# Decoder layer, attention: the mean of squares between the next tile's transposes and its product with v, the normalised output in a tile of its own

## The chip, the cores and the metric

The kernel runs on one core of one Trainium2 chip. The metric is the device time of one execution in microseconds; before the change it is 1115.36 us, the median of three runs.

## The reference, cut to what matters

The kernel computes one decoder layer on 1024 tokens of width 1024, all in float32. A combined projection feeds two mixers, a differential attention group with 4 heads and a short gated convolution; their outputs are concatenated and projected, a layer norm follows, then a gated feed-forward block with a convolution and a second layer norm. The change touches the end of the attention alone:

```python
p = jax.nn.softmax(sc, axis=-1)
a = p[:, :, 0] - lam * p[:, :, 1]
o = einsum('bhqk,bhkd->bhqd', a, v)
...
o = o * lax.rsqrt(jnp.mean(jnp.square(o), axis=-1, keepdims=True) + RMS_EPS)
o = o * attn_norm_g * (1.0 - lam_init)
```

The mean is over the 128 columns of one head, for each query.

## The kernel before

**Tiling.** The four heads follow one another (`attention(h)`, line 380). A head first gets its q and k from a projection (`project`, `pair`, lines 339 and 99). Then the queries go in four tiles of 256, `c` = 0 to 3, each of two halves of 128, `qi` = 0 and 1. A half makes both score maps (lines 448 to 450, with the causal mask added by a matmul), takes the negated row maximum on VectorE (451), the exponential on ScalarE (455), the reciprocal of the sums (460) and the difference of the two softmaxes (463 on ScalarE, 464 on VectorE). Work grows with the causal length: from 128 to 1024 keys.

**Precision.** Float32 operands are split into a rounded high part (ScalarE, line 65) and a rest (VectorE, line 66), and a product is three matmuls (74, 75, 76). A tile named with h or l at its end is such a part.

**Spread and product with v.** `spread` (409) is deferred by one half through the list `post`: it transposes the softmax difference in groups of four blocks into the one PSUM bank `tp` (415), splits each group into `pa`, and at `qi` = 1 multiplies `pa` with v into `o`, a PSUM tile of tag `pv`, which has one buffer (420 to 424). `o` is transposed output: 128 head columns by 256 queries. It is copied to `osb` (426, one buffer), and the normalisation is put on the list `rms`.

**Normalisation.** `normalise` (357) is taken from `rms` at `qi` = 1 of the next tile (`RMS_AT`, line 457); the last tile of a head waits for tile 0 of the next head, and the very last comes after everything (519). It squares `osb` on VectorE (359), splits the square into `sqh` and `sql` (65, 66), and sums over the partitions with two matmuls by a matrix of 1/128 into `mq` (364, 365), which has the same single `pv` buffer as `o`. ScalarE reads `mq` (368) and takes the inverse root by a logarithm and an exponential (370, 371). GpSimd refines it with one Newton step, multiplies it with the norm's weights and with `osb` in place (373 to 377); for the very last tile VectorE does this. SyncE's queue then writes `osb` to `cat_d` in device memory (378), from where the output projection reads it back later (597). The tiles `me` and `y` use the buffers of `sq` and `sql`; each of these tags has one buffer.

**What sets the order.** Each engine works through its own list of instructions in order. The lists are made when the program is built: a scheduler walks the program with its own idea of durations, so the order on an engine is not the order of the source. Matmuls of convolution projections (`CONV`, line 511; they are the X and Z products) stand between those of the attention. A tile is allocated anew only when its buffer's last reader is through. `after(late, early)` (line 49) adds an order between two instructions without a wait on the chip.

Of the kernel before, what the change touches and what calls it, by code (L numbers as in the profile page):

```python
# [8 lines left out]
F32 = mybir.dt.float32  # L9
# [3 lines left out]
ALU = mybir.AluOpType  # L13
# [3 lines left out]
P = 128  # L17
# [11 lines left out]
QC = 256  # L29
# [14 lines left out]
def layer_kernel(ctx: ExitStack, tc: tile.TileContext, x, xt, w_in, w_v, lam, vecs, w_out, ln, w_up, w_down, out):  # L44
    nc = tc.nc
    V, A, T, G = nc.vector, nc.scalar, nc.tensor, nc.gpsimd
    SQ = nc.sync

    def after(late, early):

        tc.add_manual_dep(late.ins, early.ins.name, mybir.DependencyInfo(
            mybir.DependencyClass.NoSync, mybir.DependencyReason.DATA), reason="order")
# [9 lines left out]
    def split(hi, lo, src, scale=None, eng=None):  # L62

        if scale is None:
            A.copy(hi, src)  # L65
            (eng or V).tensor_tensor(lo, src, hi.bitcast(F32), op=ALU.subtract)  # L66
        else:
            A.mul(hi, src, scale)
            V.scalar_tensor_tensor(lo, src, scale, hi.bitcast(F32), op0=ALU.mult, op1=ALU.subtract)
# [79 lines left out]
    cat_d = [[dram.tile([P, 512], F32, name=f"cat_d{k}_{c}") for c in range(2)] for k in range(8)]  # L149

    ident = const.tile([P, P], F32, name="ident")
# [7 lines left out]
    ones = const.tile([P, P], F32R, name="ones")  # L159
# [165 lines left out]
    at = pool("at", ab, side="right")  # L325
# [26 lines left out]
        G.memset(kl[(1 - m) * DH:(2 - m) * DH].bitcast(F32), 0.0)  # L352
        klo.append(kl)

    rms, post = [], []

    def normalise(h, c, osb):
        sq = at.tile([P, QC], F32, name="sq", tag="sq")
        V.tensor_tensor(sq, osb, osb, op=ALU.mult)
        sqh = at.tile([P, QC], F32R, name="sqh", tag="sqh")  # L360
        sql = at.tile([P, QC], F32R, name="sql", tag="sql")
        split(sqh, sql, sq)
        mq = p_pv.tile([P, 512], F32, name="mq", tag="pv", bufs=1)
        T.matmul(mq[:, :QC], ones, sqh, start=True, stop=False)
        T.matmul(mq[:, :QC], ones, sql, start=False, stop=True)

        me = at.tile([P, QC], F32, name="me", tag="sq")
        A.activation(me, mq[:, :QC], AF.Identity, bias=epsc)
        y = at.tile([P, QC], F32, name="y", tag="sql")
        A.activation(y, me, AF.Ln)  # L370
        A.activation(y, y, AF.Exp, scale=-0.5)
        E = V if (h, c) == (H - 1, S // QC - 1) else G
        E.tensor_tensor(me, me, y, op=ALU.mult)
        E.tensor_tensor(me, me, y, op=ALU.mult)
        E.tensor_scalar(me, me, gm, gp, op0=ALU.mult, op1=ALU.add)
        E.tensor_tensor(y, y, me, op=ALU.mult)
        E.tensor_tensor(osb, y, osb, op=ALU.mult)
        SQ.dma_start(cat_d[h][c // 2][:, c % 2 * QC:(c % 2 + 1) * QC], osb)

    def attention(h):  # L380

        q2 = [qk.tile([P, S], F32R, name=f"q{m}_{h}", tag=f"q{m}") for m in range(2)]
        k2 = [qk.tile([P, S], F32R, name=f"k{m}_{h}", tag=f"k{m}") for m in range(2)]

        def put_q(cs, v):
            for m in range(2):
                a_, b_ = slice(m * DH, (m + 1) * DH), slice((1 - m) * DH, (2 - m) * DH)
                A.mul(q2[m][a_, cs], v[a_], DH ** -0.5)
                V.scalar_tensor_tensor(q2[m][b_, cs], v[a_], DH ** -0.5, q2[m][a_, cs].bitcast(F32),
                                       op0=ALU.mult, op1=ALU.subtract)  # L390

        def put_k(cs, v):
            for m in range(2):
                a_, b_ = slice(m * DH, (m + 1) * DH), slice((1 - m) * DH, (2 - m) * DH)
                A.copy(k2[m][a_, cs], v[a_])
                A.copy(k2[m][b_, cs], v[a_])
                V.tensor_tensor(klo[m][a_, cs], v[a_], k2[m][a_, cs].bitcast(F32), op=ALU.subtract)

        qa, qb, ka, kb = project(h, H + h)
        put_k(c1, kb)  # L400
        put_q(c1, qb)
        put_q(c0, qa)
        put_k(c0, ka)
        vhl = at.tile([P, 2, NT, P], F32R, name=f"vhl{h}", tag="vhl")
        for c in range(2):
            SQ.dma_start(vhl[:, c].bitcast(F32), v_d[c][:, h])
        vh, vl = vhl[:, 0], vhl[:, 1]

        def spread(c, qi, pm, pa):
            i, nkb = 2 * c + qi, 2 * c + 2  # L410
            for j0 in range(0, i + 1, 4):
                nj = min(4, i + 1 - j0)
                tp = p_tr.tile([P, 4, P], F32, name="tp", tag="tr", bufs=1)
                for j in range(nj):
                    T.transpose(tp[:, j, :], pm[0][:, (j0 + j) * P:(j0 + j + 1) * P], ident)
                g = pa[j0 // 4]
                split(g[:, 0, 0:nj, qi * P:(qi + 1) * P], g[:, 1, 0:nj, qi * P:(qi + 1) * P], tp[:, :nj, :])
            if qi == 0:
                return
            o = p_pv.tile([P, 512], F32, name="o", tag="pv", bufs=1)  # L420
            for j in range(nkb):
                qs = slice(P if j == nkb - 1 else 0, QC)
                mm3(o[:, qs], vh[:, j, :], vl[:, j, :], pa[j // 4][:, 0, j % 4, qs], pa[j // 4][:, 1, j % 4, qs],
                    j == 0, j == nkb - 1, skip_group_check=True)
            osb = at.tile([P, QC], F32, name="osb", tag="osb")
            A.copy(osb, o[:, :QC])
            rms.append(lambda: normalise(h, c, osb))

        for c in range(S // QC):
            nkb = 2 * c + 2  # L430
            pa = [at.tile([P, 2, 4, QC], F32R, name=f"pa{h}_{c}_{g}", tag="pa", bufs=2) for g in range((nkb + 3) // 4)]
            for qi in range(2):
                i = 2 * c + qi
                n = (i + 1) * P
                qs = slice(i * P, (i + 1) * P)
                if post:
                    post.pop(0)()
                nm = at.tile([P, 2], F32, name="nm", tag="nm", bufs=3)
                sm = at.tile([P, 2], F32, name="sm", tag="sm", bufs=3)
                pm = []  # L440
                for m in range(2):
                    if i >= 4 or m == 0:
                        sc_ = p_sc.tile([P, S], F32, name="sc", tag="sc", bufs=2)
                    sc = sc_[:, m * 512:] if i < 4 else sc_
                    for b0 in range(0, n, 512):
                        b1 = min(n, b0 + 512)
                        bs = slice(b0, max(b1, b0 + 256))
                        T.matmul(sc[:, bs], q2[m][:, qs], k2[m][:, bs], start=True, stop=False)  # L448
                        T.matmul(sc[:, bs], q2[m][:, qs], klo[m][:, bs], start=False, stop=b1 < n)
                    T.matmul(sc[:, qs], identb, maskb, start=False, stop=True)  # L450
                    V.tensor_reduce(nm[:, m:m + 1], sc[:, :n], axis=AX.X, op=ALU.max, negate=True)  # L451
                    if i >= 4 or m == 0:
                        pt_ = at.tile([P, S], F32, name=f"p{m}", tag="p", bufs=3)
                    pt = pt_[:, m * 512:] if i < 4 else pt_
                    A.activation(pt[:, :n], sc[:, :n], AF.Exp, bias=nm[:, m:m + 1], accum_out=sm[:, m:m + 1])  # L455
                    pm.append(pt)
                if rms and (c, qi) in RMS_AT:
                    rms.pop(0)()
                rc = at.tile([P, 2], F32, name="rc", tag="rc", bufs=3)
                V.reciprocal(rc, sm)  # L460
                cc = at.tile([P, 1], F32, name="cc", tag="cc", bufs=3)
                V.tensor_tensor(cc, rc[:, 1:2], nlam, op=ALU.mult)
                A.mul(pm[0][:, :n], pm[0][:, :n], rc[:, 0:1])
                V.scalar_tensor_tensor(pm[0][:, :n], pm[1][:, :n], cc, pm[0][:, :n],  # L464
                                       op0=ALU.mult, op1=ALU.add)
                post.append(lambda c=c, qi=qi, pm=pm, pa=pa: spread(c, qi, pm, pa))

    def convolve(j):
# [44 lines left out]
    for h in range(H):  # L513
# [3 lines left out]
        if post:  # L517
            post.pop(0)()
    rms.pop(0)()
    xop_st.close()  # L520


# [142 lines left out]
    early, gates = {}, {}  # L665
# [274 lines left out]
    for j in range(HK + 2):  # L940
        if j < HK:
            op = ready.pop(0) if ready else (operand(a11[j], "S", j), operand(b11[j], "T", j))
            for t in range(4):
                mm_row(X, op, t, j == 0, j == HK - 1)
        if j >= 2:
            i = j - 2
            op = (operand(add(a21[i], a22[i], ALU.add), "S", i),
                  operand(add(b12[i], b11[i], ALU.subtract), "T", i))
# [7 lines left out]
    for t in range(4):  # L956
# [5 lines left out]
            after={2 * i: (lambda i=i: thirds(NTHIRD + i)) for i in range(HK - NTHIRD)})  # L962
# [77 lines left out]
```

## Time and profile before

| what | value |
|---|---|
| median of 3 runs | 1115.36 us (1113.97 to 1116.62) |
| the profiled execution | 1116.29 us, its span 1114.5 us |
| TensorE busy | 1082.9 us, 97% of the span, 4988 matmuls |
| VectorE busy | 890.1 us, 80% |
| ScalarE busy | 504.7 us, 45% |
| GpSimd busy | 98.7 us, 9% |
| granted TensorE clock, mean | 0.996 |

The span runs from the first to the last instruction; 1.8 us of the execution lie outside it. Busy times of different engines overlap. A wait is put down to whatever came last by the profile. TensorE's matmuls are pipelined and their ends modelled, so what counts is the time between two starts and the idle time in front of one. PE stands for TensorE's matmuls, DVE for VectorE, ACT for ScalarE, POOL for GpSimd, SPq for SyncE's queue of transfers.

### The profile page before, as it was taken

Reading aid. Unit: us, or ns where it says so; the run is one execution under the profiler, and the core shown is the slowest. Engines: PE = TensorE matmul, PEld = TensorE weight load, DVE = VectorE, ACT = ScalarE, POOL = GpSimd, SP = SyncE. Lnnn points to the kernel's source line nnn. Section 1 sums busy time; section 2 is a strip of 40 time slices with the busy share of each in tenths; the row PEclk is TensorE's granted clock in tenths of the full one; section 3 lists DMA queues with packets and bytes.
Section 4 is the critical chain, followed back from the end, with each engine's and each line's share of the span. In section 5 each row is a group of like instructions: output and inputs, shape, how many; then the busy total and the mean of one; then the engine's idle time right before and its main releaser. Section 6 shows DMA issues by size and latency. Waiting matters only on the chain.

```text
span 1114.5 us, 13774 instructions
## 1 busy us (share of the span) xinstructions
PE 1082.9 (97%) x4988; PEld 877.4 (79%) x4988; DVE 890.1 (80%) x1380; ACT 504.7 (45%) x936; POOL 98.7 (9%) x147
## 2 busy tenths in 40 slices
PE   7998999999999999999999999999999999999997
PEld 5876777877767888888888888888888887788885
DVE  7777889779888777898777777777676599997797
ACT  6357577378577421254333333333333243444540
POOL 0002313112132021200000000000000000000102
PEclk9998999999999999999999999999999999999999
DMA  7531111221213675123212122222212294120112
GB/s 265 157 94 43 43 67 39 78 74 49 81 48 112 215 256 205 42 98 126 95 57 100 71 95 76 88 83 76 95 67 85 97 397 196 39 71 34 47 66 76
DMA packets 48692, 114.32 MB, mean 103 GB/s; under 512 B 4848, under 2 KB 15216, under 8 KB 48624
## 3 DMA queue, kind: packets, MB, share of 16 engines
q1 hardware_dynamic: 48624, 113.45, 28.5%
q8 instruction: 39, 0.64, 0.2%
q14 instruction: 29, 0.24, 0.1%
HBM read 86.69 MB, written 26.74 MB: 102 GB/s over the span
## 4 chain that ended last, share of the span: by engine, by line
PE 77%; DVE 11%; ACT 4%; DMA 3%; POOL 2%; issue 2%; SPq 0%; POOLq 0%; DVEq 0%; ACTq 0%
PE X L76 9%; PE X L74 9%; PE X L75 9%; PE Z L76 5%; PE Z L74 5%; PE Z L75 5%; PE op L75 3%; PE op L74 3%; PE op L76 3%; PE dx L75 3%; PE dx L76 2%; PE dx L74 2%; PE Y L74 2%; PE Y L76 2%; PE dz L74 2%; PE dz L76 2%
## 5 line engine op out<-in xcount | busy, mean ns | idle before, releaser
L66 DVE TENSOR_TENSOR a<-s,a 128x512 fp32r<-128x512 f32 x118 | 85.4, 725 | 50.1 <-ACT a L65 49.2
L65 ACT CAST a<-s 128x512 fp32r<-128x512 f32 x118 | 73.6, 624 | 100.8 <-PE X L76 48.4
L65 ACT CAST a<-w 128x512 fp32r<-128x512 f32 x106 | 65.9, 623 | 96.9 <-PE X L76 40.3
L66 DVE TENSOR_TENSOR a<-w,a 128x512 fp32r<-128x512 f32 x106 | 74.1, 701 | 16.2 <-ACT a L65 15.9
L65 ACT CAST T<-b 128x512 fp32r<-128x512 f32 x66 | 40.7, 622 | 68.4 <-PE dz L76 33.9
L75 PE MATMUL dx<-T,S 128*128 128x512 f32 x176 | 69.1, 393 | 1.2 <-DVE T L66 1.2
L76 PE MATMUL dx<-T,S 128*128 128x512 f32 x176 | 68.6, 390 | 0.0
L74 PE MATMUL dx<-T,S 128*128 128x512 f32 x176 | 66.0, 391 | 0.0
L66 DVE TENSOR_TENSOR T<-b,T 128x512 fp32r<-128x512 f32 x66 | 45.3, 689 | 16.6 <-ACT T L65 16.6
L451 DVE TENSOR_REDUCE nm<-sc 128x1 f32<-128x128 f32 (+5 forms) x64 | 47.5, 751 | 6.2 <-PE sc L450 5.7
L75 PE MATMUL dz<-T,S 128*128 128x512 f32 x132 | 51.8, 392 | 0.0
L76 PE MATMUL dz<-T,S 128*128 128x512 f32 x132 | 51.5, 390 | 0.0
L74 PE MATMUL op<-wo,c 128*128 128x512 f32 x128 | 50.6, 395 | 0.0
L455 ACT ACTIVATE p<-sc,nm 128x128 f32<-128x128 f32 (+5 forms) x64 | 47.5, 743 | 6.3 <-DVE p L464 3.8
L76 PE MATMUL op<-wo,c 128*128 128x512 f32 x128 | 50.0, 390 | 0.0
L75 PE MATMUL op<-wo,c 128*128 128x512 f32 x128 | 50.0, 390 | 0.0
L74 PE MATMUL dz<-T,S 128*128 128x512 f32 x132 | 48.4, 394 | 0.5 <-ACT T L65 0.4
L810 ACT ACTIVATE t<-t 128x1024 f32<-128x1024 f32 x22 | 23.4, 1062 | 50.7 <-DVE t L809 50.7
L448 PE MATMUL sc<-k,q 128*128 128x512 f32 (+2 forms) x96 | 37.1, 394 | 5.4 <-ACT p L455 4.6
L75 PEld LDWEIGHTS dx<-T,S 128*128 128x128 f32 x176 | 33.0, 188 | 9.7 <-DVE T L66 2.9
L74 PEld LDWEIGHTS dx<-T,S 128*128 128x128 f32 x176 | 33.0, 188 | 7.4 <-ACT T L65 0.6
L76 PEld LDWEIGHTS dx<-T,S 128*128 128x128 f32 x176 | 33.1, 188 | 6.7
(318 smaller groups left out, 3229.9 us busy)
## 6 DMA issues: line engine op xcount, KB each, us to landing
w<-in_w_up SPq DMA_DIRECT2D x44, 512.0 KB, 3.3
b<-in_w_down SPq DMA_DIRECT2D x44, 256.0 KB, 6.6
w<-in_w_in SPq DMA_DIRECT2D x20, 512.0 KB, 3.4
act_d<-act SPq DMA_DIRECT2D x19, 512.0 KB, 2.6
ra<-act_d SPq DMA_DIRECT2D x19, 512.0 KB, 7.1
v_d<-vs SPq DMA_DIRECT2D x16, 256.0 KB, 2.7
vhl<-v_d SPq DMA_DIRECT2D x8, 512.0 KB, 4.7
wo_r<-in_w_out SPq DMA_DIRECT2D x8, 512.0 KB, 3.9
```

Of the source, the lines that this page charges most:

```text
L65: A.copy(hi, src)
L66: (eng or V).tensor_tensor(lo, src, hi.bitcast(F32), op=ALU.subtract)
L74: T.matmul(ps, lh, rh, start=first, stop=False, **kw)
L75: T.matmul(ps, lh, rl, start=False, stop=False, **kw)
L76: T.matmul(ps, ll, rh, start=False, stop=last, **kw)
L448: T.matmul(sc[:, bs], q2[m][:, qs], k2[m][:, bs], start=True, stop=False)
L451: V.tensor_reduce(nm[:, m:m + 1], sc[:, :n], axis=AX.X, op=ALU.max, negate=True)
L455: A.activation(pt[:, :n], sc[:, :n], AF.Exp, bias=nm[:, m:m + 1], accum_out=sm[:, m:m + 1])
L810: A.activation(t_, t_, AF.Silu)
```

## The change

The normalisation is cut in two. `squares` makes `sq`, `sqh` and `sql` where `normalise` stood. The rest goes on a second list, `means`, and is taken from it inside the next `spread` with `qi` = 1, right after the first group of transposes, with an order that puts the first `mq` matmul behind the last of these transposes. In the source, its ScalarE and GpSimd work now comes ahead of the split of that group. The product with `osb` is now the first of the five GpSimd instructions and writes a new tile `on`, which has the one buffer of `sqh`; the last multiplies `on` by the refined factor, and the transfer reads `on`.

```diff
-    def normalise(h, c, osb):
+    def squares(h, c, osb):
         sq = at.tile([P, QC], F32, name="sq", tag="sq")
         V.tensor_tensor(sq, osb, osb, op=ALU.mult)
         sqh = at.tile([P, QC], F32R, name="sqh", tag="sqh")
         sql = at.tile([P, QC], F32R, name="sql", tag="sql")
         split(sqh, sql, sq)
+        means.append(lambda early=None: normalise(h, c, osb, sqh, sql, early))
+
+    def normalise(h, c, osb, sqh, sql, early):
         mq = p_pv.tile([P, 512], F32, name="mq", tag="pv", bufs=1)
-        T.matmul(mq[:, :QC], ones, sqh, start=True, stop=False)
+        first = T.matmul(mq[:, :QC], ones, sqh, start=True, stop=False)
+        if early is not None:
+            after(first, early)
...
         E = V if (h, c) == (H - 1, S // QC - 1) else G
+        on = at.tile([P, QC], F32, name="on", tag="sqh")
+        E.tensor_tensor(on, y, osb, op=ALU.mult)
         E.tensor_tensor(me, me, y, op=ALU.mult)
         E.tensor_tensor(me, me, y, op=ALU.mult)
         E.tensor_scalar(me, me, gm, gp, op0=ALU.mult, op1=ALU.add)
-        E.tensor_tensor(y, y, me, op=ALU.mult)
-        E.tensor_tensor(osb, y, osb, op=ALU.mult)
-        SQ.dma_start(cat_d[h][c // 2][:, c % 2 * QC:(c % 2 + 1) * QC], osb)
+        E.tensor_tensor(on, on, me, op=ALU.mult)
+        SQ.dma_start(cat_d[h][c // 2][:, c % 2 * QC:(c % 2 + 1) * QC], on)
...
                 for j in range(nj):
-                    T.transpose(tp[:, j, :], pm[0][:, (j0 + j) * P:(j0 + j + 1) * P], ident)
+                    last = T.transpose(tp[:, j, :], pm[0][:, (j0 + j) * P:(j0 + j + 1) * P], ident)
+                if qi == 1 and means:
+                    means.pop(0)(last)
...
-            rms.append(lambda: normalise(h, c, osb))
+            rms.append(lambda: squares(h, c, osb))
...
     rms.pop(0)()
+    means.pop(0)()
```

## Rows read from the trace of the kernel before

**Rows 1.** Page, part 1: busy time, share of the span, instructions.
```profile
PE   1082.9 (97%) x4988; PEld 877.4 (79%) x4988; DVE 890.1 (80%) x1380; ACT 504.7 (45%) x936; POOL 98.7 (9%) x147
```
**Rows 2.** Busy time by stretch: PE, PEld, DVE, ACT, POOL; clock; DMA share; GB/s.
```profile
85.00:385.00 300.00, 286.94 (x1452) 225.51 (x1451) 250.11 (x423) 198.39 (x416) 65.23 (x78) 0.99 0.21 73
102.20:105.69 3.49, 0.00 (x1) 0.00 (x0) 1.22 (x2) 1.99 (x4) 0.00 (x0) 0.86 0.54 188
105.69:111.60 5.91, 5.91 (x17) 4.64 (x18) 4.04 (x7) 2.55 (x6) 0.00 (x0) 0.50 0.00 0
197.00:213.00 16.00, 16.00 (x70) 12.89 (x69) 11.19 (x16) 5.51 (x10) 1.95 (x3) 1.00 0.22 74
370.00:400.00 30.00, 30.00 (x134) 24.74 (x133) 21.91 (x32) 5.07 (x8) 1.90 (x2) 1.00 0.57 215
```
**Rows 3.** Waits, 75 to 385 us: total us, times, longest us.
```profile
PE sc L448 <- ACT p L455: 4.6, 5, 1.5
PE mq L364 <- ACT sqh L65: 3.9, 2, 3.5
ACT osb L426 <- DMA cat_d<-osb: 11.3, 6, 3.4
DVE s L117 <- DMA w<-in_w_in: 1.0, 2, 0.5
```
**Rows 4.** Timeline, head 0, tiles 0 and 1: start us, duration us, engine.
```profile
92.44 0.28 PE L364 MATMUL mq<-sqh,ones 128*128 128x256 f32 x1
...
95.79 1.14 POOL L373 TENSOR_TENSOR me<-me,y 128x256 f32<-128x256 f32 x1 [51.53 <-DVE rc L460]
...
98.49 2.52 POOL L376 TENSOR_TENSOR y<-y,me 128x256 f32<-128x256 f32 x1
...
101.08 0.73 POOL L377 TENSOR_TENSOR osb<-y,osb 128x256 f32<-128x256 f32 x1
...
101.84 0.33 SPq L378 DMA_DIRECT2D cat_d<-osb  x1
...
103.66 0.37 ACT L426 COPY osb<-o 128x256 f32<-128x256 f32 x1 [3.37 <-DMA cat_d<-osb]
...
105.69 0.58 PE L364 MATMUL mq<-sqh,ones 128*128 128x256 f32 x1 [3.49 <-ACT sqh L65]
```
**Rows 5.** Timeline of PE: the other idle times behind a late osb.
```profile
121.30 0.55 PE L415 MATMUL tp<-ident,p 128*128 128x128 f32 x3 [0.65 <-DVE pa L66]
...
179.83 0.50 PE L448 MATMUL sc<-k,q 128*128 128x512 f32 x1 [1.43 <-ACT p L455]
...
263.26 0.39 PE L364 MATMUL mq<-sqh,ones 128*128 128x256 f32 x1 [0.46 <-ACT sqh L65]
...
334.71 0.50 PE L448 MATMUL sc<-k,q 128*128 128x512 f32 x1 [1.55 <-ACT p L455]
```
**Rows 6.** Groups of instructions, 85 to 385 us: busy us, mean ns; idle before.
```profile
L377 POOL TENSOR_TENSOR osb<-y,osb 128x256 f32<-128x256 f32 x15 | 14.6, 971 | 1.2
L368 ACT ACTIVATE me<-mq,epsc 128x256 f32<-128x256 f32 x16 | 7.6, 477 | 2.2 <-PE mq L365 2.1
L370 ACT ACTIVATE y<-me 128x256 f32<-128x256 f32 x16 | 6.7, 421 | 0.3
L377 DVE TENSOR_TENSOR osb<-y,osb 128x256 f32<-128x256 f32 x1 | 0.4, 419 | 0.0
```
**Rows 7.** Timeline, head 1: transposes of tiles 0, 1 and 2, and tile 1's loop.
```profile
161.53 0.38 PE L415 MATMUL tp<-ident,p 128*128 128x128 f32 x2
...
167.77 0.38 PE L415 MATMUL tp<-ident,p 128*128 128x128 f32 x2
...
180.39 0.28 PE L364 MATMUL mq<-sqh,ones 128*128 128x256 f32 x1
...
182.86 0.60 PE L415 MATMUL tp<-ident,p 128*128 128x128 f32 x4
...
188.97 0.36 ACT L426 COPY osb<-o 128x256 f32<-128x256 f32 x1
```

More of the change, by code (lines that the diff above doesn't have):

```diff
@@ L353, in layer_kernel @@
         klo.append(kl)
-    rms, post = [], []
-    def normalise(h, c, osb):
+    rms, means, post = [], [], []
+    def squares(h, c, osb):
         sq = at.tile([P, QC], F32, name="sq", tag="sq")
```

## The prediction

> **What bounds the kernel now.** I read the busy times first: TensorE is busy 97% of the span, the next engine 80% [rows 1]. So time is lost or won where TensorE stands still or runs slowly. The stretches come next: attention, from 85 to 385 us, leaves TensorE idle for 300 - 286.9 = 13.1 us [rows 2]. That, and what the clock loses, is all that a reordering inside attention can win.
>
> The waits say who ends this idle time: scores that wait for an exponential (4.6 us) and the mean's matmul that waits for `sqh` (3.9 us) [rows 3]. Behind both stands one wait on ScalarE: six copies of `o` to `osb` wait 11.3 us in all until the last tile's output has left the one `osb` buffer [rows 3]. ScalarE works in order, so exponentials and splits queue behind such a copy.
>
> The timeline shows it in full in head 0. The mean of tile 0 starts at 92.44, GpSimd starts at 95.79 and needs until 101.81, the write goes out at 101.84, and the copy of tile 1, which waited 3.37 us, runs at 103.66. TensorE has the mean's matmul next in its list and idles 3.49 us [rows 4]. Then the granted clock is 0.50 from 105.69 to 111.60, the lower of its two levels (1.2 of 2.4 GHz): 5.91 us of work that takes 2.95 us at the full clock [rows 2]. The other copies cost TensorE 0.65, 1.43, 0.46 and 1.55 us [rows 5]. The chain thus costs TensorE 3.49 + 4.09 = 7.58 us of idle time (0.67 us per us of ScalarE's wait) and 2.95 us of clock: **10.5 us** of the profiled 1116.29 us, which stands 0.9 us above the median of 1115.36.
>
> **What the change removes.** `osb` is now read for the last time by GpSimd's first instruction, not by the write behind the fifth. A mean of GpSimd's multiplication is 0.97 us [rows 6]; the buffer comes free some 6.0 - 1.1 + 1.8 = 6.7 us earlier after the root is there [rows 4]. Against that the mean starts later, behind the next tile's transposes. I take it that the wait for `osb` goes in all six places: -10.5 us, bounds -10.5 and 0.
>
> **What it adds.** The buffers are still single, so the loop from mean to mean remains, with its wait in another place. `on` stands in the buffer of `sqh` until it is written out, and `me` in that of `sq` until GpSimd's last instruction. So VectorE's next square waits for GpSimd, and ScalarE's next `sqh` for the write. Behind the square stand row maxima and splits, behind `sqh` exponentials and splits; TensorE waits for all of these. The two waits are one, as the write follows GpSimd's last instruction by 1.8 us [rows 4].
>
> From a mean to the freed buffer it was 103.66 - 92.44 = 11.2 us in head 0, with the copy's wait, and 188.97 - 180.39 = 8.6 us at most in head 1, without one [rows 4, 7]. With the split behind it, two instructions of about 0.4 us (as VectorE's multiplication of the same shape [rows 6]), the new loop is 9.4 to 12.0 us. The means now follow the transposes, and in head 1 those of tiles 0, 1 and 2 stand 6.2 and 15.1 us apart [rows 7]. So from tile 0 to tile 1 the loop is longer than the gap, in heads 1 to 3 (head 0 has no tile before its first); from tile 1 to 2 it is shorter, except in head 0, where the two are near. The product of tile 1 comes 3 to 6 us later there, since it needs the `pv` buffer after the mean. The X and Z matmuls can cover that where the list has them in its place; TensorE pays for what the list did not foresee. Four such places, priced at the 1.43 us of head 1, which is nearest in kind, cost **5.7 us** (bounds 0 and four times 3.49, 14.0).
>
> GpSimd sets the loop's length. The same multiplication takes 0.73 us once and 2.52 us another time, 0.97 us in the mean [rows 4, 6]. The Trainium skill, GPSIMD Engine Reference, section Performance versus the Vector engine, gives 2.6 cycles an element for two inputs, which makes an estimate of 0.55 us for these 256 elements at its 1.2 GHz; five would end 3.2 us earlier than the 6.0 us of head 0, and with the new waits gone the sum would be -9.2 us. By the rows most of the six waits would then not exist before the change either, so I keep to the rows.
>
> The product also waits for ScalarE to read `mq` out of the shared buffer: 16 times 0.48 us [rows 6], 7.6 us without cover. If ScalarE ran the root ahead of the split of the transposes, it would be 0.48 + 0.42 + 0.42 = 1.3 us each time, 21 us in all. The split's input is there before the mean is, and X and Z matmuls can stand in the gap; I take a sixth of 7.6, **1.3 us**, bounds 0 and 7.6.
>
> **What costs nothing.** The counts of matmuls, ScalarE and GpSimd instructions stay. The writes move some 4 us back in SyncE's queue, past loads of weights; these cost VectorE 1.0 us in all now [rows 3], so I take 0, and up to 2 us if that cover is gone. The last tile's root stays at the end, where TensorE is busy 30.0 of 30.0 us [rows 2]. The handovers into tile 3 fall under projections (TensorE 16.0 of 16.0 us, ScalarE 5.5 [rows 2]).
>
> **Sum:** -10.5 + 5.7 + 1.3 = **-3.5 us**, so 1112.8 for the profiled execution and 1111.9 for the median. What is late next is GpSimd's last instruction and the write.
>
> **The rivals.** *The single buffer decides (slower).* Every handover now meets its buffer late, since each mean starts right before the next product; before, ten of sixteen copies did not wait. Of 15 handovers 4 lie under projections. Eleven, at 11.3/6 = 1.88 us on ScalarE and 0.67 on TensorE, cost 13.9 us: 3.4 us more than the 10.5 saved, and 6.3 with one fall of the clock as in head 0. That is 1118.8 to 1121.7, say 1120. It decides from nine such waits on (9 times 1.26 is 11.3). For it speaks that `on` lives longer than the old `osb` past the next product; against it, that the mean's matmul no longer stands right behind the split. The Trainium skill, Perfetto Trace Analysis, section Optimization Strategy, says that consistent bubbles can mean too few buffers for the next tile; by that rule the wait stays, as no buffer is added. The trace bears it out for `osb`, in six of sixteen copies.
>
> *The wait only moves.* The copies' 11.3 us turn up on `sq` and `sqh` with about the same price, and head 0's stall stays in some form: 1115.4.
>
> *All of it goes.* The lists have cover for each late buffer: -10.5 + 1.3 = -9.2 us, 1106.2. Against it speak the 6.2 us gaps in three heads.
>
> That the change does nothing is excluded: the product must follow the mean in the one `pv` buffer, so the mean does sit between transposes and product.
>
> **How the numbers follow.** My forecast has 0.42, the single buffer 0.26, the moved wait 0.24, all gone 0.08. A measurement of this kernel tells some 0.2% (2.2 us) from no change. The forecast's own range is 1109 to 1113.3, from two new waits of 1.43 us to five, nearly all of it faster; most outcomes of the moved wait lie within 0.2%. That makes faster 0.47, same 0.26, slower 0.27. The range of 1106 to 1120.5 leaves out the far half of the first rival and what lies below the last. The likeliest value is 1111.9.
>
> **What would show it.** Right: no ScalarE wait of `osb` for a write; TensorE at the full clock from 100 to 115 us; waits of `sqh` for the write of `cat_d` and of `sq` for GpSimd, few and below 2 us; attention's idle time near 10 us. Wrong: an `mq` or score matmul that idles over 3 us behind `sqh`, a clock of 0.5 anywhere in attention, or a product with v that waits for `me` in most tiles.

## The result, and the profile after

The changed kernel takes **1133.51 us** (median of 4 runs, 1131.40 to 1135.53), the kernel before 1115.21 us beside it: a ratio of 1.0163, interval 1.0150 to 1.0175. That is 18 us slower, where 3.5 us faster was forecast, and outside the range. The profiled execution took 1135.53 us, its span 1133.7 us.

The page's busy times, to be held against [rows 1]: the work is the same, the span longer. TensorE's idle time over the whole span (span less busy time) grows from 31.6 to 46.7 us, and the same 4988 matmuls are busy 4.1 us longer.

```profile
PE 1087.0 (96%) x4988; PEld 879.5 (78%) x4988; DVE 886.6 (78%) x1380; ACT 503.9 (44%) x936; POOL 103.9 (9%) x147
```

The stretch of attention by itself, from 60 to 400 us, first of the kernel before (columns as in [rows 2]):

```profile
60.00:400.00 340.00, 326.18 (x1621) 256.06 (x1622) 278.03 (x469) 215.54 (x451) 67.14 (x80) 0.99 0.24 84
```

and the same stretch after, with eight microseconds of head 1:

```profile
60.00:400.00 340.00, 310.16 (x1538) 241.36 (x1538) 263.16 (x455) 213.64 (x449) 71.57 (x78) 0.98 0.21 69
178.00:186.00 8.00, 6.84 (x23) 5.54 (x24) 5.66 (x10) 3.82 (x8) 0.04 (x1) 0.57 0.05 16
```

TensorE's idle time in it grows from 340 - 326.2 = 13.8 to 340 - 310.2 = 29.8 us, by 16.0 us; the granted clock falls a little more (0.98 against 0.99). That is most of the 19.2 us between the two profiled spans. The waits of the kernel after, from 75 to 410 us, say where it comes from (columns as in [rows 3]):

```profile
PE tp L421 <- DVE pa L66: 11.2, 8, 3.0
PE sc L456 <- ACT p L463: 6.1, 7, 1.9
ACT sqh L65 <- DMA cat_d<-on: 17.9, 10, 2.8
DVE sq L359 <- POOL on L383: 21.0, 11, 2.8
DVE s L117 <- DMA w<-in_w_in: 8.0, 4, 2.7
```

ScalarE's copies to `osb` no longer wait for a write, as forecast; four of them wait 2.0 us in all for GpSimd's first instruction. But VectorE's square now waits 21.0 us for GpSimd's last instruction, and ScalarE's `sqh` 17.9 us for the write: 38.9 us in 21 waits, where there were 11.3 us in 6. A wait of 3.9 us that TensorE's mean had is gone; eight waits of the transposes for the split of the group before stand there now (11.2 us; two and 1.2 us before). VectorE's wait for weights grows from 1.0 to 8.0 us.

One of these in the timeline, head 1:

```profile
169.75 0.36 PE L367 MATMUL mq<-sqh,ones 128*128 128x256 f32 x1
...
174.66 0.37 ACT L434 COPY osb<-o 128x256 f32<-128x256 f32 x1 [0.48 <-POOL on L379]
...
177.32 0.72 POOL L383 TENSOR_TENSOR on<-on,me 128x256 f32<-128x256 f32 x1
...
178.07 0.42 DVE L359 TENSOR_TENSOR sq<-osb 128x256 f32<-128x256 f32 x1 [2.83 <-POOL on L383]
...
178.42 0.68 DVE L66 TENSOR_TENSOR pa<-tp,pa 128x512 fp32r<-128x512 f32 x1
...
179.16 0.47 PE L421 MATMUL tp<-ident,p 128*128 128x128 f32 x1 [3.00 <-DVE pa L66]
```

This is to be read from below. TensorE stands 3.00 us before a transposition, since the one `tp` bank is still being split by VectorE. That split is quick (0.68 us), but it stands behind the square in VectorE's list. The square has its input since the copy at 174.66, but its buffer still holds `me`, which GpSimd reads last in the instruction from 177.32 to 178.04. That is the end of the chain of the mean that began at 169.75: copy and square of the next tile come up before this chain is through. A piece of work that nobody needs for another tile holds up one that TensorE needs now. From 178 to 186 us the clock is granted at 0.57, most of it at the lower level.

### The profile page after: what moved, and what is told of

Same layout as the page of the kernel before. It is cut to its first block, busy times and chain, and to the rows that moved or that the text cites. A ratio compares the mean times of both kernels' runs of the same rounds, so it can differ in the third digit from the quotient of the medians.

```text
span 1133.7 us, 13765 instructions
## 1 busy us (share of the span) xinstructions
PE 1087.0 (96%) x4988; PEld 879.5 (78%) x4988; DVE 886.6 (78%) x1380; ACT 503.9 (44%) x936; POOL 103.9 (9%) x147
## 4 chain that ended last, share of the span: by engine, by line
PE 71%; DVE 11%; POOL 5%; DMA 5%; ACT 5%; issue 2%; SPq 0%; POOLq 0%; DVEq 0%; ACTq 0%
PE X L74 8%; PE X L75 8%; PE X L76 8%; PE Z L74 5%; PE Z L75 5%; PE Z L76 5%; PE op L75 3%; PE op L76 3%; PE op L74 3%; PE dx L75 2%; PE dx L76 2%; PE dx L74 2%; PE Y L75 2%; PE dz L75 2%; PE Y L74 2%
## 5 line engine op out<-in xcount | busy, mean ns | idle before, releaser
L66 DVE TENSOR_TENSOR a<-s,a 128x512 fp32r<-128x512 f32 x118 | 82.5, 700 | 48.8 <-ACT a L65 47.7
L75 PEld LDWEIGHTS dx<-T,S 128*128 128x128 f32 x176 | 33.1, 188 | 9.5 <-DVE T L66 2.8
L379 POOL TENSOR_TENSOR on<-y,osb 128x256 f32<-128x256 f32 x15 | 16.4, 1095 | 253.9 <-ACT y L376 86.8
L421 PE MATMUL tp<-ident,p 128*128 128x128 f32 x144 | 25.1, 284 | 15.1 <-DVE pa L66 11.2
```

The source lines that it names most:

```text
L75: T.matmul(ps, lh, rl, start=False, stop=False, **kw)
L379: E.tensor_tensor(on, y, osb, op=ALU.mult)
L421: last = T.transpose(tp[:, j, :], pm[0][:, (j0 + j) * P:(j0 + j + 1) * P], ident)
```

## The experiments

Theory A: the shared single buffers are late, because the mean starts a tile later. B: the place itself costs. C: the tile `on` is the fault wherever the mean stands. D: the moved writes hold up the loads. Ratios are to the kernel before on the same chip; where space for a tile was needed, an unused scratch area was cut.

An edit also lets the scheduler order the lists anew. So for some runs the lists of VectorE (1380 instructions) and ScalarE (936) are compared from the traces; a pair of numbers, as 9 and 2, says how many instructions of each stand outside the order that the two kernels share.

### The two halves of the change

The second half alone: the mean in its old place, the five GpSimd instructions and the write as in the change.

```diff
         E = V if (h, c) == (H - 1, S // QC - 1) else G
+        on = at.tile([P, QC], F32, name="on", tag="sqh")
+        E.tensor_tensor(on, y, osb, op=ALU.mult)
...
-        E.tensor_tensor(y, y, me, op=ALU.mult)
-        E.tensor_tensor(osb, y, osb, op=ALU.mult)
+        E.tensor_tensor(on, on, me, op=ALU.mult)
```

> The kernel before, with the second half of the change alone: the product with osb first and into on, in the buffer of sqh; the mean stands in its old place, right behind the split of the squares. Theory A (a buffer is late because the mean starts a tile later): the mean is early, so its buffers come free before the next copy nearly as they did: 1110 to 1118 us. Theory C (the tile on is the fault wherever the mean stands): 1124 to 1133 us. Theory B says the same as A here.

Measured: 1112.06 us, ratio 0.9962 (0.9948 to 0.9976). The same waits are there, but small. Of ScalarE and VectorE in this kernel:

```profile
ACT sqh L65 <- DMA cat_d<-on: 6.3, 3, 2.5
DVE sq L359 <- POOL on L378: 3.5, 4, 1.1
```

The first half alone: the mean moved, the output in place.

```diff
-        on = at.tile([P, QC], F32, name="on", tag="sqh")
-        E.tensor_tensor(on, y, osb, op=ALU.mult)
...
-        E.tensor_tensor(on, on, me, op=ALU.mult)
+        E.tensor_tensor(y, y, me, op=ALU.mult)
+        E.tensor_tensor(osb, y, osb, op=ALU.mult)
```

(against the changed kernel)

> The change with the first half alone: the mean between transposes and product, the output in place in osb as before. Theory A: osb, sq and their copies wait for a write that starts a tile later: at least as slow as the whole change, 1131 to 1145 us. Theory B: 1130 to 1135 us. Theory C: 1113 to 1120 us.

Measured: 1138.24 us, ratio 1.0200 (1.0185 to 1.0216). The old wait, that of ScalarE's copy, has nearly four times its size, in 14 of 16 copies:

```profile
ACT osb L433 <- DMA cat_d<-osb: 41.3, 14, 7.5
```

So the two halves have opposite signs, and they add up: +2.00% and -0.38% make 1.62%, and the whole change has 1.63%. Theory C falls.

### One buffer freed at a time

```diff
-        on = at.tile([P, QC], F32, name="on", tag="sqh")
+        on = at.tile([P, QC], F32, name="on", tag="on")
...
-    nc = _bacc.Bacc("TRN2", target_bir_lowering=False, num_devices=1, dynamic_dma_scratch_size=1024)
+    nc = _bacc.Bacc("TRN2", target_bir_lowering=False, num_devices=1, dynamic_dma_scratch_size=256)
```

> The change, with on in a buffer of its own (1 KB a partition; the unused scratch of GpSimd's transfers is cut by 768 B to make room). Theory A (the new waits are on the shared buffers; the dearer one is VectorE's square, which waits for GpSimd's last instruction because me stands in its buffer): the 17.9 us of ScalarE for the write of on go, the 21.0 us of VectorE stay, 1124 to 1131 us. Theory B (the place alone costs it: the product with v waits for the mean in the one PSUM buffer): no gain, 1130 to 1135 us. Theory C (the write of on is the dear wait): near the kernel before, 1113 to 1119 us.

Measured: 1126.98 us, ratio 1.0097 (1.0082 to 1.0112). ScalarE's wait for the write is gone; VectorE's stays to the digit (21.0 us, 11 times).

The other one, with the same cut of scratch:

```diff
-        me = at.tile([P, QC], F32, name="me", tag="sq")
+        me = at.tile([P, QC], F32, name="me", tag="me")
```

> The change, with me in a buffer of its own and on still in that of sqh (same cut of scratch). Theory A: the square no longer waits for GpSimd, ScalarE's wait for the write of on stays, 1117 to 1125 us, better than with on alone set free. Theory B: 1130 to 1135 us. Theory C: 1128 to 1134 us.

Measured: 1129.47 us, ratio 1.0124 (1.0108 to 1.0139), a miss: I had expected this to bring more than `on`. Its lists are nearly those of the change (9 and 2; with `on` freed 33 and 24), so these 4.4 us (0.39%) come from the buffer. The square is free, but now ScalarE meets the write in nearly every tile:

```profile
ACT sqh L65 <- DMA cat_d<-on: 27.1, 15, 3.6
```

The two waits stand one behind the other on the way to the next mean. Freeing one lets the work run into the other, so neither run shows what both cost. The next one does.

### All shared buffers free, in both places

`on` in its own buffer, and GpSimd works on it alone after the first product, with the same five shapes; the Newton step is left out. The first kernel is the change with this edit, the second, its control, has the mean in the old place.

```diff
-        E.tensor_tensor(me, me, y, op=ALU.mult)
-        E.tensor_tensor(me, me, y, op=ALU.mult)
-        E.tensor_scalar(me, me, gm, gp, op0=ALU.mult, op1=ALU.add)
-        E.tensor_tensor(on, on, me, op=ALU.mult)
+        E.tensor_tensor(on, on, on, op=ALU.mult)
+        E.tensor_tensor(on, on, on, op=ALU.mult)
+        E.tensor_scalar(on, on, gm, gp, op0=ALU.mult, op1=ALU.add)
+        E.tensor_tensor(on, on, on, op=ALU.mult)
```

> The change with every shared buffer free early: on in its own buffer, and GpSimd works on that tile alone after the first product (five instructions of the same shapes; the Newton step is left out: on is squared twice, scaled by gm plus gp and squared again), so me and y are read for the last time at the root and at GpSimd's first instruction. The mean stays between transposes and product. Theory A (the place costs through the late buffers): VectorE's and ScalarE's waits of sq and sqh for GpSimd and the write go, 1110 to 1118 us. Theory B (the place costs by itself: the product waits for the mean and its reading in the one PSUM buffer, the mean for the product before): still 1123 to 1131 us.

> The control of the run with all shared buffers free: the same short-lived tiles and the same GpSimd work (Newton step left out in the same way), with the mean in its old place. The place by itself is then this run against that one. If the place costs nothing once the buffers are free: 1110 to 1114 us. If the product's wait for the mean in the one PSUM buffer has a price of its own: 1103 to 1108 us, 4 us or more below it.

Measured: 1112.60 us, ratio 0.9969 (0.9958 to 0.9980), in the moved place; 1102.69 us, ratio 0.9888 (0.9873 to 0.9903), in the old, just below its second range. The place costs 2.0% with shared buffers (1.0163 - 0.9962) and 0.8% with free ones (0.9969 - 0.9888): some 22 us, of which the late buffers are 13 and something else is 9. The 13 us are an estimate: they rest on four runs, and from the change to the first kernel the lists differ too (63 and 48). Theory A has the larger part, B or D the rest. VectorE's waits of the first kernel, from 75 to 410 us, hint at which:

```profile
DVE s L117 <- DMA w<-in_w_in: 11.0, 4, 4.6
DVE sq L359 <- ACT osb L434: 2.6, 5, 1.0
```

and of the control:

```profile
DVE s L117 <- DMA w<-in_w_in: 3.2, 3, 2.0
```

The square no longer waits for GpSimd in either, but for the copy to `osb` (in the control 4.6 us, 3 times). What differs most is the wait for weights. No matmul waits for ScalarE's reading of the mean in either; TensorE's operand loads ahead of the product (PEld) wait for it 2.3 us in all, 8 times, in the first kernel and never in the control.

### The write in another queue

```diff
-        SQ.dma_start(cat_d[h][c // 2][:, c % 2 * QC:(c % 2 + 1) * QC], on)
+        G.dma_start(cat_d[h][c // 2][:, c % 2 * QC:(c % 2 + 1) * QC], on)
```

(against the changed kernel)

> The change, with the write of on issued by GpSimd's queue right behind its last instruction, so that no load of weights stands behind it in SyncE's queue. Theory A: the loads are late because their own buffers come free late, not because of the queue: 1130 to 1136 us, VectorE's wait for weights stays near 8 us. Theory D (the moved writes hold up the loads): VectorE's wait for weights falls to 1 or 2 us and the time to 1122 to 1128 us.

Measured: 1142.68 us, ratio 1.0241 (1.0225 to 1.0256), outside both ranges. ScalarE's and VectorE's waits, from two answers:

```profile
ACT sqh L65 <- DMA cat_d<-on: 35.5, 11, 5.4
```
```profile
DVE s L117 <- DMA w<-in_w_in: 4.2, 3, 2.6
```

The wait for weights falls by half (8.0 to 4.2 us), between what A and D had named, but the writes land later from this queue and `sqh` waits twice as long. So the time says nothing of D, and the wait speaks for it only in part. For A the run says more than it was made for: the lists are nearly those of the change (11 and 6), the buffer of `sqh` comes free later, and the kernel is 0.78% slower (1.0241 - 1.0163, 8.7 us).

### Which mean holds up the next head

Each of these puts one mean of a head back in its old place, in the kernel with the free buffers and the moved mean. The edit shown is the first; the second has `c == 3` in place of `c == 2`.

```diff
         means.append(lambda early=None: normalise(h, c, osb, sqh, sql, early))
+        if c == 2 and (h, c) != (H - 1, S // QC - 1):
+            means.pop(0)()
```

> The run with all shared buffers free and the mean moved, with the mean of tile 2 of each head alone back in its old place. There the moved mean of tile 2 comes 27 us later in head 1, after the convolution's projections, and its write stands at the head's end next to the loads for the next head. If that delays the next head's weights: VectorE's wait for weights falls from 11 us to 3 to 6 us and the time from 1112.6 to 1104 to 1108 us. If not: 1110 to 1113 us.

> The same with the mean of tile 3 of each head alone back in its old place, at tile 0 of the next head. If the late mean of tile 3 holds up the next head's first product: 1104 to 1108 us. If it is tile 2 or the place in general: 1110 to 1113 us.

Measured: tile 2 back, 1107.69 us, ratio 0.9935 (0.9920 to 0.9950); tile 3 back, 1109.79 us, ratio 0.9956 (0.9939 to 0.9973). The first time lies in its range, but the kernel before takes 1114.87 us on this chip and 1116.23 us on that of the kernel with all means moved; the second lies between its two ranges. By the ratios tile 2 wins 0.34% of the 0.81%, and VectorE's wait for weights falls below the 3 to 6 us that I had expected:

```profile
DVE s L117 <- DMA w<-in_w_in: 2.1, 3, 0.9
```

In the timelines the copies of `osb` tell where. From the last copy of a head to the first of the next it was 31.3, 32.5 and 32.9 us with all means moved, 28.6, 29.9 and 29.6 us with tile 2 back, and 29.3, 28.9 and 29.4 us in the control. So with the mean of tile 2 back, the stretch between heads is nearly that of the control, and the weights come in time. With tile 3 back it is 30.2, 31.4 and 30.2 us, so that mean has a part in it too.

The queue shows how the weights come late. In SyncE's list the loads of the next head's v and weights stand behind the write of tile 2. With all means moved that write goes out late, the v loads are issued 1.8, 1.5 and 1.0 us after the last copy of a head, and the first weights behind them land 10.3, 9.4 and 9.9 us after it. With tile 2 back, and in the control, the v loads are issued at the copy, within 0.2 us, and the weights land 6.5 to 7.8 us after it. From all means moved to tile 2 back only 20 of TensorE's 4988 matmuls stand in another order, the means among them. That is theory D, for this part of the place. Tile 3 back wins 0.13%, which its interval doesn't tell from nothing. The other 0.3% or more stay open: the rest of the place, without a name.

### A longer loop

```diff
         E.tensor_scalar(me, me, gm, gp, op0=ALU.mult, op1=ALU.add)
+        E.tensor_tensor(me, me, y, op=ALU.mult)
+        E.tensor_tensor(me, me, y, op=ALU.mult)
```

(against the changed kernel)

> The change with two more GpSimd multiplications on me before the last one (the output is scaled by the square of the root in addition): the loop from mean to freed buffers grows by 1.5 to 2.3 us, nothing else. Theory A: each of some 11 late squares waits as much longer, VectorE's wait of 21 us grows to 35 to 45 us, 1140 to 1155 us. Theory B (the buffers are not what costs): 1132 to 1136 us.

Measured: 1153.39 us, ratio 1.0337 (1.0315 to 1.0360), 20 us above the change. ScalarE's and VectorE's waits, from two answers:

```profile
ACT sqh L65 <- DMA cat_d<-on: 37.9, 12, 4.8
```
```profile
DVE sq L359 <- POOL on L385: 34.7, 13, 3.9
```

GpSimd's own time, on an engine that is busy 9% of the span, goes into the total: the two new instructions take 11.7 and 11.0 us in 15 tiles, and 20 us come out as time. The lists differ as well (58 and 37), so not all of it need be the loop; but the waits grew where theory A had said, VectorE's just short of its 35 us. The loop from the mean to the freed buffers sets the pace here.

### The old place, with buffers

Four kernels with the mean in its old place. The first is the kernel before with the cut scratch alone:

> The kernel before with the unused scratch of GpSimd's transfers cut from 1024 to 256 B and nothing else: every theory says no change, 1114 to 1118 us; any other time would have to be taken off the runs that use this cut.

Measured: 1115.38 us, ratio 1.0000 (0.9991 to 1.0010): nothing is to be taken off. The second adds one buffer to it:

```diff
-            osb = at.tile([P, QC], F32, name="osb", tag="osb")
+            osb = at.tile([P, QC], F32, name="osb", tag="osb", bufs=2)
```

> The kernel before with two buffers for osb and nothing else changed. Theory A: the copies' wait for the write goes (11.3 us on ScalarE), VectorE's square waits for GpSimd now and then: 1107 to 1114 us. If the waits of osb are covered anyway: 1114 to 1118 us.

The third has the second half of the change, with `tag="on"` in place of `tag="sqh"`:

> The mean in its old place, the product with osb first, and on in a buffer of its own: the wait of sqh for the write goes too. Theory A: a little better than with on in sqh's buffer, 1108 to 1113 us; it should beat both kernels. Theory C: 1124 us or more.

The fourth is the third, with `me` in the buffer of `sqh` in place of that of `sq`:

```diff
-        me = at.tile([P, QC], F32, name="me", tag="sq")
+        me = at.tile([P, QC], F32, name="me", tag="sqh")
```

> The best version so far, the mean in its old place and on in its own buffer, with me moved from the buffer of sq to that of sqh, which is free once the mean is taken: VectorE's square no longer waits for GpSimd (4.3 us there), ScalarE's sqh may wait for it instead. 1103 to 1107 us if such waits still cost; the same as without it, 1105 to 1107 us, if they are covered.

Measured: two buffers of `osb`, 1106.68 us, ratio 0.9915 (0.9901 to 0.9930). `on` in its own, 1106.04 us, ratio 0.9909 (0.9892 to 0.9925). With `me` moved as well, **1103.98 us, ratio 0.9902 (0.9885 to 0.9918)**. The first two are just below their ranges. The last two aren't told apart by their intervals; all three beat both kernels. All of them have the lists of the second half alone, save 4 instructions of VectorE with two buffers of `osb`. TensorE's list is the same too. So giving `on` its own buffer is worth 0.53% (0.9962 - 0.9909, 5.9 us) by the buffer alone; against the kernel before, the lists differ too (57 to 61 and 31). The stretch from 60 to 400 us of the last, with 5.2 us of idle time where 13.8 us were, and the full clock:

```profile
60.00:400.00 340.00, 334.80 (x1683) 265.75 (x1683) 283.78 (x484) 218.59 (x456) 74.56 (x84) 1.00 0.26 91
```

## Why the prediction was wrong

**What bounds the kernel** was read rightly. The chain behind the one `osb` buffer was priced at 10.5 us; the kernels that free it without moving the mean win 9.55 us (1116.23 - 1106.68) and 10.2 us (1116.23 - 1106.04), the order of their lists included. In the change the copies' waits fell from 11.3 to 2.0 us, so this term stands, near enough.

**The step that failed** is the new waits: "Four such places, priced at the 1.43 us of head 1, ... cost 5.7 us (bounds 0 and four times 3.49, 14.0)". There were not four such places: each of the 15 handovers has a late square, a late `sqh` or both, 11 squares and 10 `sqh` in all, and these 21 waits are 38.9 us on VectorE and ScalarE. The gap between two means was the wrong thing to hold the loop against. A square is put in VectorE's list soon after the copy of `o`, and the copy follows the mean of the tile before at once, now that the mean stands right before the product. In the trace the next copy comes 3.6 to 8.4 us after a mean starts and GpSimd is through 6.7 to 9.4 us after it: in all 15 handovers the copy comes first. In the kernel before the copy came 8.6 to 30.7 us after the mean, and always after GpSimd. So nearly every square now comes up before its buffer is free, whether or not the next mean is far off. The rule was in the text, as the first rival: "Every handover now meets its buffer late, since each mean starts right before the next product". I gave it 0.26, and weighed against it that the mean no longer stands behind the split. That relieves TensorE of a wait for the mean, but not the row maxima and splits behind the square.

**"The two waits are one"** failed as well. They follow each other, but on two engines with different work behind them. Freed singly, `on` gives back 7.4 us (0.66%) and `me` 4.4 us (0.39%); freed together they give 21.6 us (1.0163 - 0.9969), of which 8.3 us come in the old place too (0.9962 - 0.9888).

**The price per microsecond** was nearly right. TensorE's idle time grew by 16.0 us while 7.58 us went: 23.6 us new, where the sum had 5.7. On 38.9 us of waits that is 0.61 against the 0.67 of the sum, so it was the number of late places that was wrong. Part of that is luck: the idle time behind the 8.0 us of waits for weights is in it too, and the new waits have other work behind them. The rival's 3.4 to 6.3 us were too small for the number and the kind of its waits.

**"The writes move some 4 us back ... I take 0, and up to 2 us"** failed too. VectorE waits 8.0 us for weights, from 1.0 [rows 3]. I had moved all means by one distance. In head 1 that of tile 2 now follows the convolution's projections: with free buffers it stands 32.7 us behind that of tile 1, and 9.4 us with tile 2 put back; in the other heads the move is some 4 us, as I had said. In all three gaps between heads its write then goes out ahead of the loads and late. Putting it back brings 0.34%.

**The product's wait for the mean** (1.3 us, bounds 0 and 7.6) isn't to be seen as such: no matmul of the product waits for `me` in any run here. The operand loads ahead of it do, 1.9 us in 6 places of the change, and none in the old place; what that costs isn't shown.

**Of the signs** of being right, two came: no copy waits for a write, and the clock is full from 100 to 115 us. Two did not: the waits of `sq` and `sqh` are 21 and up to 2.8 us long, and TensorE is idle 28.5 us from 85 to 385 us, where about 10 was expected. Of the signs of being wrong one came: the clock is 0.50 from 179.16 to 185 us.

The Trainium skill, Perfetto Trace Analysis, section Optimization Strategy, says that consistent bubbles can mean too few buffers. The runs agree: one buffer more wins 9.55 us in the old place. The Trainium skill's GPSIMD Engine Reference, section Performance versus the Vector engine, would have made an instruction 0.55 us (an estimate from its 2.6 cycles an element, for 256 elements at its 1.2 GHz). The first two of GpSimd's groups of the changed kernel differ from it (busy us, mean ns; idle before):

```profile
L380 POOL TENSOR_TENSOR me<-me,y 128x256 f32<-128x256 f32 x15 | 17.1, 1141 | 0.0
L379 POOL TENSOR_TENSOR on<-y,osb 128x256 f32<-128x256 f32 x15 | 16.4, 1095 | 253.9 <-ACT y L376 86.8 <-PE sc L458 58.3 <-DVE pa L66 54.4
```

They take twice that, and the quickest of the five, the last, takes 0.76 us in the mean. Here the measured time decides. The longer loop shows that time of GpSimd goes into the total; what this difference is worth isn't shown, since no run makes GpSimd faster.

## What to carry to other kernels

A buffer that two steps share ties the second step to the last reader of the first: before work is moved later, list each tile that stands in a shared buffer, its last reader, and when the next writer comes up in its engine's list. What waits there is not what needs the buffer but all that is queued behind it. Free the buffer first, and then see whether there is still anything to move: here the freed buffer, with the lists that came with it, won 0.9% without the move, and the move lost 2% with shared buffers and still 0.8% with free ones.

## What the runs showed of the hardware that was not expected

GpSimd's product with `osb` takes 0.97 us in the mean before, as the last of its five instructions [rows 6], and 1.10 us after, as the first; the last of the five takes 0.76 us there. A write issued by GpSimd lands in 2.0 us in the median, up to 5.2 us, where SyncE's lands in 1.7 us, up to 2.2 us. The granted clock fell to the lower level around a wait of TensorE of 3.49 us before [rows 2, 4] and one of 3.00 us in the change, and fell, too, behind the change's other long wait, 3.01 us in head 3 (0.78 from 348.38 to 356 us); around the waits of 1.43 and 1.55 us before [rows 5] it was granted in full (1.00 from 176 to 181 and from 331 to 336 us).
